# Sums of weight tiles started one item sooner, with one written order for VectorE's weight work

## The chip, the cores and the metric

The kernel runs on one core of a Trainium2 chip. The metric is the device time of one launch in microseconds, lower is better; times are medians over runs of the same kernel.

## The reference

A decoder trunk of two layers over x, 256 tokens of 2048 features in f32. Layer 0 uses differential attention, layer 1 latent attention; each layer then attends into 256 memory tokens and ends with a squared-ReLU MLP, which is the place of the change:

```python
def sq_relu_mlp(h, wup, wdown):        # wup 2048 x 8192, wdown 8192 x 2048
    return jnp.square(jax.nn.relu(h @ wup)) @ wdown

for i in range(2):
    x = x + attention_i(rms_norm(x, attn_norm[i]))
    x = x + memory_cross_attention(rms_norm(x, cross_norm[i]), mem_h, ca_wq[i], ca_wkv[i], ca_wo[i])
    x = x + sq_relu_mlp(rms_norm(x, mlp_norm[i]), mlp_wup[i], mlp_wdown[i])
return rms_norm(x, final_norm)
```

## The kernel before

**Three matmuls for one.** Every large product is made of three TensorE passes in the type fp32r. A weight tile and an activation tile are each split into a hi part (a cast to fp32r) and a lo part (what the cast lost); the passes are hi by hi, hi by the weights' lo, and the activations' lo by hi. Activations split in this way lie in "units", tiles of 128 partitions by hi and lo by 4 x 256 numbers, from the pool `units` with 13 places.

**The way of a weight tile.** All weights come in tiles of 1 MB, 128 partitions by 2048 f32 numbers (`raw`, pool `wraw`, 6 places of 8 KB in a partition; a unit takes 8 KB too). SP's queue issues the loads, in the order in which the program writes them (L165). ScalarE casts a half of a tile (128x1024) to `whi` (L193), and VectorE subtracts it from the raw half to make `wlo` (L194). There are four buffers for each of these two halves. So a tile needs two casts and two lo parts, and TensorE uses each half as soon as its lo part is there.

**The list of tiles.** `plan` is the list of all tiles in the order of their use. `take()` hands the next one to TensorE's code and calls `fill()`, which keeps four items written ahead: for each it writes the load, the casts and the lo parts into the program.

**The MLP.** The 8192 hidden columns are cut into 8 blocks of 1024. Block 0 is multiplied by the up weights in the plain way. Blocks 1 to 7 go through `Seven`: a block is seen as 2 x 2 blocks of smaller matrices, and seven products of sums of blocks replace eight plain products. They are worked in the order p1, p5, p3, p7, p2, p6, p4. A product takes two tiles, x = 0 and 1, of 12 matmuls each. The sums on the side of the activations are made by `Forms` and don't change here. Those on the side of the weights are made in the raw tiles themselves:

- p1, p3 and p2 use a fetched tile as it is (block 00, 11 or 10 of the up weights).
- p5 uses p1's tile plus a newly fetched one (block 01), and p7 uses p3's tile plus that same one. These two sums are VectorE's (L758, one instruction of 128x2048, in place). They are called "the sums" below: two tiles, two products, seven blocks and two layers make 56.
- p6 and p4 use what p7 and p6 leave, and add a block by a DMA that accumulates in place, issued from POOL's queue (L764) after the lo parts of p7 or p6.

**The order of the items.** `mlp_line` weaves tiles of the down projection between those of the products, and each down tile feeds 24 matmuls. The pattern is first tile of a product, second tile, down tile. In blocks 2 to 6 there is one more down tile between the two tiles of p3. The last product of a block, p4, is held back and stands between p1 and p5 of the next block, as a pair of its own with its down tile. A product's matmuls write PSUM banks named `pr`, those of the down projection `mm`.

**What sets the order on each engine.** TensorE's instructions stay as the program writes them. For the other engines a list scheduler sets the order when the kernel is built, from a model of durations: among the instructions whose inputs it reckons ready it takes those written first. Instructions under `keep_in_program_order` (loads, accumulating DMAs, the sums) keep their written order in their own queue. The lo parts are not so tied. Once built, each engine works strictly in its order.

Of the kernel before, what the change touches and what calls it, by code (L numbers as in the profile page):

```python
# [14 lines left out]
ALU = mybir.AluOpType  # L15
# [6 lines left out]
CH = 512  # L22
EPS = 1e-6
WARM = 13
RAWS = 6
MLP_BLOCKS = 8
SEVEN = (1, 2, 3, 4, 5, 6, 7)
EVS = 7
# [17 lines left out]
def trunk(ctx, tc, x, xT, mem, memT, positions, gcols, gfinal, lam_vecs, consts, W, out):  # L46
    nc = tc.nc

    def pool(name, bufs, space=None):
        kw = {"space": space} if space else {}  # L50
        return ctx.enter_context(tc.tile_pool(name=name, bufs=bufs, **kw))

    keep = pool("keep", 1)
    wraw = pool("wraw", RAWS)
    whalf = pool("whalf", 4)
    units = pool("units", 13)
    work = pool("work", 2)
    small = pool("small", 3)
    banks = pool("banks", 8, bass.MemoryType.PSUM)
# [3 lines left out]
    def nm(s):  # L63
        serial[0] += 1
        return f"{s}_{serial[0]}"
# [13 lines left out]
    class Task:  # L79
# [9 lines left out]
        def step(self):  # L89
            try:  # L90
                d = next(self.gen)
            except StopIteration:
                self.done = True
                side.remove(self)
                return
            if isinstance(d, Task):
                self.waits = d
            else:
                self.waits = None
                self.ready = clock[0] + d  # L100
# [60 lines left out]
    def f32(ap):  # L161
        return ap.bitcast(F32)
# [2 lines left out]
        tc.keep_in_program_order((queue or nc.sync).dma_start(dst, src))  # L165


    stream = []

    def raw_tile():  # L170
        return wraw.tile([P, 4 * CH], F32, tag="raw", name=nm("raw"))
# [1 line left out]
    def split_weights(src, width, pieces=2, loads=1, queue=None):  # L173
        raw = raw_tile()
        n = 4 * width
        m = n // loads
        for i in range(loads):
            load(raw[:, i * m : (i + 1) * m], src[:, i * m : (i + 1) * m], queue)
        return halves_of(raw, n, pieces)

    class split_pieces:
# [4 lines left out]
        def next(self):  # L186
            m, i = self.m, self.i
            at = i * m % (self.n // 2)
            if at == 0:
                self.halves.append([whalf.tile([P, 2 * CH], F32R, tag=tag, name=nm(tag)) for tag in ("whi", "wlo")])  # L190
            hi, lo = (w[:, at : at + m] for w in self.halves[-1])
            r = self.raw[:, i * m : (i + 1) * m]
            nc.scalar.copy(hi, r)  # L193
            nc.vector.tensor_tensor(lo, r, f32(hi), ALU.subtract)  # L194
            self.i += 1

    def halves_of(raw, n=4 * CH, pieces=2):
# [4 lines left out]

    plan = []
    ready = []
    AHEAD = 4

    def fill():
        while len(ready) < AHEAD and plan:
            job = plan.pop(0)
            if callable(job):  # L210
                ready.append(job())
            else:
                name, i, width = job
                ready.append(split_weights(W[name][i, :, : 4 * width], width))
# [4 lines left out]
    def take():  # L219
        fill()  # L220
        got = ready.pop(0)
        fill()
        taken[0] += 1
        if taken[0] in hooks:
            hooks[taken[0]]()
        return got
# [496 lines left out]
    class Seven:  # L723
# [18 lines left out]
            return raw  # L742

        def job(self, p, x):
            def run():
                r, other = self.raw, None
                if p in self.B:
                    o = r[p, x] = self.fetch(*self.B[p], x)
                elif p == "p5":
                    o, other = r.pop(("p1", x)), self.fetch(0, 1, x)  # L750
                    r["12", x] = other
                elif p == "p7":
                    o, other = r.pop(("p3", x)), r.pop(("12", x))
                else:
                    o = r.pop((p, x))
                split = split_pieces(o, 4 * CH, 2)
                if other is not None:
                    tc.keep_in_program_order(nc.vector.tensor_tensor(o, o, other, ALU.add))  # L758
                for _ in range(2):
                    split.next()  # L760
                if p in self.ADDED:
                    after, block = self.ADDED[p]
                    r[after, x] = o
                    add = nc.gpsimd.dma_start(o, self.source(*block, x), accum_op=ALU.add)  # L764
                    tc.keep_in_program_order(add)
                return split.halves

            return run

        def items(self):  # L770
# [611 lines left out]
def build(a, w):  # L1382
    import concourse.bacc as bacc

    nc = bacc.Bacc("TRN2", target_bir_lowering=False, num_devices=1, dynamic_dma_scratch_size=1024)
    arrays = {}

    def dram(name, v):
        arrays[f"in_{name}_dram"] = v
        return nc.dram_tensor(f"in_{name}_dram", v.shape, mybir.dt.from_np(v.dtype), kind="ExternalInput").ap()  # L1390

    args = [dram(k, a[k]) for k in ("x", "xT", "mem", "memT", "positions", "gcols", "gfinal", "lam_vecs", "consts")]
    weights = {k: dram(k, v) for k, v in w.items()}
    o = nc.dram_tensor("out_0_dram", (S, D), F32, kind="ExternalOutput").ap()
    with tile.TileContext(nc, schedule_with_timeline_sim=True) as tc, tc.manual_schedule(engines={mybir.EngineType.PE}):
        trunk(tc, *args, weights, o)
    return nc, arrays
# [8 lines left out]
```

## Time and profile before

| | |
|---|---|
| median of 3 runs (lowest to highest) | 2247.47 us (2247.27 to 2249.18) |
| the profiled execution, and its span | 2249.26 us, 2247.5 us |
| granted TensorE clock, mean | 0.998 |
| TensorE matmul / weight load busy | 2228.2 us (99%) / 1853.7 us (82%) |
| VectorE busy | 1675.6 us (75%) |
| ScalarE busy | 1354.6 us (60%) |
| GpSimd busy | 153.9 us (7%) |
| moved from and to memory | 484.09 MB, 215 GB/s on average |

Three groups of instructions belong to the weights:

```profile
L194 DVE TENSOR_TENSOR wlo<-raw,whi 128x1024 fp32r<-128x1024 f32 (+2 forms) x962 | 1154.6, 1213 | 483.6 <-ACT whi L193 455.2
L193 ACT CAST whi<-raw 128x1024 fp32r<-128x1024 f32 (+2 forms) x962 | 993.6, 1041 | 754.5 <-PE mm L155 530.9
L758 DVE TENSOR_TENSOR raw<-raw,raw 128x2048 f32<-128x2048 f32 x56 | 127.9, 2284 | 0.0
```

Such a row names line, engine and operation, what is written from what, how many there are, then the busy time in us and the mean of one in ns, and last the idle time of the engine just ahead of them and what ended most of it. PE is TensorE, PEld its loading of the stationary operand, DVE is VectorE, ACT ScalarE, POOL GpSimd, SP the queue that issues the loads. In a row of the timeline the first two numbers are start and length in us, xN says that N instructions stand in the row, and the bracket names an idle time ahead of it and what ended that. In a row of the waits stand the engine that waited and for what, then us in total, number of waits and the longest.

### The profile page before, as it was taken

To read this page: it belongs to the slowest core of one execution; us is meant where nothing else is said; L and a number is where in the kernel's file an instruction comes from. 1 tells how busy PE (TensorE), PEld (TensorE's weight loads), DVE (VectorE), ACT (ScalarE), POOL (GpSimd) and SP (SyncE) were. 2 spreads that over 40 slices of the span, in tenths; PEclk is the share of its full clock that TensorE was granted. 3 is DMA by queue.
4 is the path that set the end of the run, shared out by engine and by line. 5 is a ranking of instruction groups with operands and counts; after the bars stand their busy time and mean duration, and the time that the engine had idled before them with its cause. 6 is when DMAs were issued, how large, how long until landed. Compare 5 with 4: busy or idle time off the path is not lost.

```text
span 2247.5 us, 27444 instructions
## 1 busy us (share of the span) xinstructions
PE 2228.2 (99%) x10521; PEld 1853.7 (82%) x10521; DVE 1675.6 (75%) x1836; ACT 1354.6 (60%) x1815; POOL 153.9 (7%) x250
## 2 busy tenths in 40 slices
PE   9999999999999999999999999999999999999998
PEld 7888888888888888888889888888888888888786
DVE  6665647678888788788765766778887887887864
ACT  6544645666666666656655755566666666666664
POOL 0210110000000000000000311000000000000001
PEclk9999999999999999999999999999999999999999
DMA  9446555435877877876955334643688678678692
GB/s 364 157 143 210 193 197 206 152 129 206 262 250 254 244 249 255 244 249 219 297 176 180 116 141 150 243 150 132 216 255 277 222 250 275 223 250 276 221 306 75
DMA packets 73716, 484.09 MB, mean 215 GB/s; under 512 B 8432, under 2 KB 8816, under 8 KB 18032
## 3 DMA queue, kind: packets, MB, share of 16 engines
q1 hardware_dynamic: 64944, 422.56, 50.9%
q0 software_dynamic: 8064, 58.72, 13.1%
q8 instruction: 82, 1.34, 0.2%
q10 hardware_dynamic: 576, 1.05, 0.2%
q14 instruction: 50, 0.41, 0.1%
HBM read 480.20 MB, written 2.10 MB: 215 GB/s over the span
## 4 chain that ended last, share of the span: by engine, by line
PE 92%; DVE 5%; ACT 2%; issue 1%; DMA 0%; ACTq 0%; POOLq 0%
PE mm L155 66%; PE pr L155 20%; PE ax L155 3%; PE ax L159 2%; DVE wlo L194 2%; DVE raw L758 2%; ACT whi L193 1%; PE mm L159 1%; DVE unit L289 0%; DMA raw<-in_da_wqkv_dram 0%; DVE x L438 0%; DVE unit L316 0%; ACT ev L1078 0%; DVE unit L487 0%; DVE os L658 0%
## 5 line engine op out<-in xcount | busy, mean ns | idle before, releaser
L194 DVE TENSOR_TENSOR wlo<-raw,whi 128x1024 fp32r<-128x1024 f32 (+2 forms) x962 | 1154.6, 1213 | 483.6 <-ACT whi L193 455.2
L193 ACT CAST whi<-raw 128x1024 fp32r<-128x1024 f32 (+2 forms) x962 | 993.6, 1041 | 754.5 <-PE mm L155 530.9
L155 PE MATMUL mm<-whi,unit 128*128 128x512 f32 (+3 forms) x4544 | 1444.0, 389 | 2.6 <-ACT unit L315 1.7
L155 PEld LDWEIGHTS mm<-whi,unit 128*128 128x128 f32 x4544 | 850.1, 188 | 169.2 <-ACT unit L315 2.7
L155 PE MATMUL mm<-wlo,unit 128*128 128x512 f32 (+3 forms) x2272 | 878.3, 387 | 2.2 <-DVE wlo L194 2.2
L155 PE MATMUL pr<-whi,unit 128*128 128x512 f32 x1568 | 502.9, 391 | 0.0
L155 PEld LDWEIGHTS mm<-wlo,unit 128*128 128x128 f32 x2272 | 428.0, 188 | 85.6 <-DVE wlo L194 7.2
L155 PEld LDWEIGHTS pr<-whi,unit 128*128 128x128 f32 x1568 | 294.4, 188 | 61.3 <-ACT whi L193 0.5
L155 PE MATMUL pr<-wlo,unit 128*128 128x512 f32 x784 | 307.3, 392 | 3.0 <-DVE wlo L194 2.7
L155 PEld LDWEIGHTS pr<-wlo,unit 128*128 128x128 f32 x784 | 147.2, 188 | 39.5 <-DVE wlo L194 9.5
L758 DVE TENSOR_TENSOR raw<-raw,raw 128x2048 f32<-128x2048 f32 x56 | 127.9, 2284 | 0.0
L764 POOL DMA_DIRECT2D raw<-in_mlp_wup_dram x56 | 49.4, 882 | 1125.6 <-DVE wlo L194 990.3
L438 DVE TENSOR_TENSOR x<-x,mm 128x512 f32<-128x512 f32 x152 | 100.0, 682 | 9.4 <-PE mm L155 8.7
L328 POOL TENSOR_TENSOR rs<-rs,mhalf 128x1 f32<-128x1 f32 (+1 forms) x28 | 23.5, 844 | 681.5 <-DVE rs L327 681.5
L288 ACT CAST unit<-ax 128x512 fp32r<-128x512 f32 (+1 forms) x88 | 48.9, 567 | 30.1 <-PE ax L159 27.7
L289 DVE TENSOR_TENSOR unit<-ax,unit 128x512 fp32r<-128x512 f32 (+1 forms) x88 | 57.4, 661 | 3.0 <-ACT unit L288 1.3
L500 ACT ACTIVATE p<-ax,nmax 128x256 f32<-128x256 f32 (+1 forms) x80 | 33.6, 428 | 30.0 <-DVE nmax L498 29.5
L322 ACT ACTIVATE junk<-x 128x512 bf16<-128x512 f32 x56 | 35.2, 628 | 9.4 <-DVE x L438 8.4
L155 PE MATMUL ax<-unit,unit 128*128 128x256 f32 (+1 forms) x240 | 37.2, 281 | 0.0
L155 PEld LDWEIGHTS ax<-unit,unit 128*128 128x128 f32 x240 | 34.3, 190 | 2.5
L155 PE MATMUL ax<-raw,unit 128*128 128x256 f32 (+1 forms) x240 | 35.3, 279 | 0.8 <-ACT unit L486 0.6
L155 PEld LDWEIGHTS ax<-raw,unit 128*128 128x128 f32 x240 | 32.0, 190 | 2.4 <-ACT unit L486 1.0
(150 smaller groups left out, 925.8 us busy)
## 6 DMA issues: line engine op xcount, KB each, us to landing
raw<-in_mlp_wup_dram SPq DMA_DIRECT2D x128, 1024.0 KB, 5.0
raw<-in_mlp_wdown_dram SPq DMA_DIRECT2D x128, 1024.0 KB, 7.0
raw<-in_mlp_wup_dram POOLq DMA_DIRECT2D x56, 1024.0 KB, 11.0
raw<-in_da_wqkv_dram SPq DMA_DIRECT2D x45, 1024.0 KB, 5.0
raw<-in_da_wo_dram SPq DMA_DIRECT2D x16, 1024.0 KB, 4.9
raw<-in_ca_wkv_dram SPq DMA_DIRECT2D x16, 1024.0 KB, 4.9
raw<-in_mla_wo_dram SPq DMA_DIRECT2D x16, 1024.0 KB, 5.0
raw<-in_ca_wq_dram SPq DMA_DIRECT2D x8, 1024.0 KB, 5.1
```

Of the source, the lines that this page charges most:

```text
L155: return nc.tensor.matmul(o, stationary, moving, start=start, stop=stop, skip_group_check=not alone)
L159: nc.tensor.transpose(o, src, ident)
L193: nc.scalar.copy(hi, r)
L194: nc.vector.tensor_tensor(lo, r, f32(hi), ALU.subtract)
L288: nc.scalar.copy(hi, src)
L289: nc.vector.tensor_tensor(dst[:, 1, :n, t * P : (t + 1) * P], src, f32(hi), ALU.subtract)
L322: nc.scalar.activation(junk[:, : src.shape[1]], src, AF.Square, accum_out=acc)
L328: nc.gpsimd.tensor_tensor(r[:, :n], r[:, :n], mhalf.broadcast_to([P, n]), ALU.pow)
L438: nc.vector.tensor_tensor(xc, xc, ps, ALU.add)
L500: nc.scalar.activation(pr[:, i * w : (i + 1) * w], sb[:, i * w : (i + 1) * w], AF.Exp, bias=nmax[:, i : i + 1], accum_out=ssum[:, i : i + 1],)
L758: tc.keep_in_program_order(nc.vector.tensor_tensor(o, o, other, ALU.add))
L764: add = nc.gpsimd.dma_start(o, self.source(*block, x), accum_op=ALU.add)
```

## The change

It has four parts.

1. An item of `Seven` is cut in two. `begin()` fetches its tile and writes the sum, `run()` the casts, the lo parts and the accumulating DMA. `fill()` calls `begin()` of the next item before it writes the current one. So a product's load and sum stand one item sooner in the program; for the second tile of p5 and p7 that is ahead of the first tile's casts and lo parts, and for the first tile ahead of the preceding down tile's load, casts and lo parts.
2. Every lo part and every sum gets the same issue order token, "weights" (`in_turn`). All lo parts and sums then have one order among themselves on VectorE, the written one; before, the sums had one only among themselves.
3. `wraw` has 7 places instead of 6.
4. `units` has 12 places instead of 13, so the two pools together take the same room.

```diff
-RAWS = 6
+RAWS = 7
...
-    units = pool("units", 13)
+    units = pool("units", 12)
...
+    def in_turn(ins):
+        tc.stamp_issue_order_token(ins.ins, "weights")
+        return ins
...
             nc.scalar.copy(hi, r)
-            nc.vector.tensor_tensor(lo, r, f32(hi), ALU.subtract)
+            in_turn(nc.vector.tensor_tensor(lo, r, f32(hi), ALU.subtract))
             self.i += 1
...
     def fill():
         while len(ready) < AHEAD and plan:
             job = plan.pop(0)
+            if callable(job) and job not in begun:
+                job.begin()
+            if plan and callable(plan[0]):
+                begun.append(plan[0])
+                plan[0].begin()
             if callable(job):
                 ready.append(job())
...
         def job(self, p, x):
-            def run():
+            def begin():
                 r, other = self.raw, None
                 if p in self.B:
-                    o = r[p, x] = self.fetch(*self.B[p], x)
+                    r[p, x] = self.fetch(*self.B[p], x)
                 elif p == "p5":
-                    o, other = r.pop(("p1", x)), self.fetch(0, 1, x)
+                    r[p, x], other = r.pop(("p1", x)), self.fetch(0, 1, x)
                     r["12", x] = other
                 elif p == "p7":
-                    o, other = r.pop(("p3", x)), r.pop(("12", x))
-                else:
-                    o = r.pop((p, x))
+                    r[p, x], other = r.pop(("p3", x)), r.pop(("12", x))
+                if other is not None:
+                    in_turn(nc.vector.tensor_tensor(r[p, x], r[p, x], other, ALU.add))
+
+            def run():
+                o = self.raw[p, x]
                 split = split_pieces(o, 4 * CH, 2)
-                if other is not None:
-                    tc.keep_in_program_order(nc.vector.tensor_tensor(o, o, other, ALU.add))
                 for _ in range(2):
                     split.next()
                 if p in self.ADDED:
                     after, block = self.ADDED[p]
-                    r[after, x] = o
+                    self.raw[after, x] = o
                     add = nc.gpsimd.dma_start(o, self.source(*block, x), accum_op=ALU.add)
                     tc.keep_in_program_order(add)
                 return split.halves
 
+            run.begin = begin
             return run
```

By the added lines the lo part's line becomes L196, the sum's L763, and the lines behind them move likewise (L289 is L297, L793 is L803). TensorE's and POOL's orders are unchanged.

**VectorE at p5 of block 2 (layer 0), before.** Here and in the next two places `raw` is a weight tile, `whi` and `wlo` its halves, `unit` a down tile's activations, `u` a row of sums of products; numbers are the kernel's own names, which differ between the two kernels. raw_5109 is p5's first tile, raw_5144 its second, raw_5261 the down tile ahead of p5:

```order
L194 TENSOR_TENSOR wlo_5246<-raw_4799,whi_5245 128x1024
L289 TENSOR_TENSOR unit_5192<-ax_5329,unit_5192 128x4x128
L758 TENSOR_TENSOR raw_5144<-raw_5144,raw_5337 128x2048
L194 TENSOR_TENSOR wlo_5264<-raw_5261,whi_5263 128x1024
L194 TENSOR_TENSOR wlo_5268<-raw_5261,whi_5267 128x1024
L758 TENSOR_TENSOR raw_5109<-raw_5109,raw_5287 128x2048
L793 TENSOR_TENSOR u_1009_5188<-pr_5336,u_1009_5188 128x512
L194 TENSOR_TENSOR wlo_5291<-raw_5109,whi_5290 128x1024
```

The same place in the change, where raw_5081 is p5's first tile, raw_5111 its second and raw_5264 the down tile:

```order
L196 TENSOR_TENSOR wlo_5246<-raw_4766,whi_5245 128x1024
L763 TENSOR_TENSOR raw_5081<-raw_5081,raw_5261 128x2048
L297 TENSOR_TENSOR unit_5192<-ax_5332,unit_5192 128x4x128
L196 TENSOR_TENSOR wlo_5267<-raw_5264,whi_5266 128x1024
L196 TENSOR_TENSOR wlo_5271<-raw_5264,whi_5270 128x1024
L763 TENSOR_TENSOR raw_5111<-raw_5111,raw_5290 128x2048
L803 TENSOR_TENSOR u_1009_5188<-pr_5339,u_1009_5188 128x512
L196 TENSOR_TENSOR wlo_5294<-raw_5081,whi_5293 128x1024
```

The two sums keep their two places but for one row, and change them with each other: the first tile's stands ahead of the down tile's lo parts, the second tile's behind them.

**VectorE at p7 of block 1, before.** raw_4764 is p7's first tile, raw_4799 its second, raw_4821 the down tile ahead of p7:

```order
L194 TENSOR_TENSOR wlo_4806<-raw_4799,whi_4805 128x1024
L194 TENSOR_TENSOR wlo_4824<-raw_4821,whi_4823 128x1024
L194 TENSOR_TENSOR wlo_4828<-raw_4821,whi_4827 128x1024
L758 TENSOR_TENSOR raw_4764<-raw_4764,raw_4674 128x2048
L289 TENSOR_TENSOR unit_4880<-ax_4930,unit_4880 128x4x128
L194 TENSOR_TENSOR wlo_4847<-raw_4764,whi_4846 128x1024
L194 TENSOR_TENSOR wlo_4851<-raw_4764,whi_4850 128x1024
L758 TENSOR_TENSOR raw_4799<-raw_4799,raw_4717 128x2048
L289 TENSOR_TENSOR unit_4880<-ax_4967,unit_4880 128x4x128
L194 TENSOR_TENSOR wlo_4888<-raw_4799,whi_4887 128x1024
```

And in the change, where the three tiles are raw_4740, raw_4766 and raw_4822:

```order
L196 TENSOR_TENSOR wlo_4806<-raw_4766,whi_4805 128x1024
L763 TENSOR_TENSOR raw_4740<-raw_4740,raw_4633 128x2048
L196 TENSOR_TENSOR wlo_4825<-raw_4822,whi_4824 128x1024
L196 TENSOR_TENSOR wlo_4829<-raw_4822,whi_4828 128x1024
L763 TENSOR_TENSOR raw_4766<-raw_4766,raw_4677 128x2048
L196 TENSOR_TENSOR wlo_4848<-raw_4740,whi_4847 128x1024
L196 TENSOR_TENSOR wlo_4852<-raw_4740,whi_4851 128x1024
L297 TENSOR_TENSOR unit_4881<-ax_4932,unit_4881 128x4x128
L196 TENSOR_TENSOR wlo_4888<-raw_4766,whi_4887 128x1024
```

The first sum moves ahead of the down tile's two lo parts, the second ahead of the first tile's two.

**VectorE at p5 of block 1, before.** The down tile ahead of p5 is raw_4633; the sums are of raw_4556, p5's first tile, and raw_4590, its second:

```order
L289 TENSOR_TENSOR unit_4625<-ax_4667,unit_4625 128x4x128
L758 TENSOR_TENSOR raw_4556<-raw_4556,raw_4674 128x2048
L194 TENSOR_TENSOR wlo_4593<-raw_4590,whi_4592 128x1024
L289 TENSOR_TENSOR unit_4625<-ax_4703,unit_4625 128x4x128
L194 TENSOR_TENSOR wlo_4597<-raw_4590,whi_4596 128x1024
L194 TENSOR_TENSOR wlo_4636<-raw_4633,whi_4635 128x1024
L758 TENSOR_TENSOR raw_4590<-raw_4590,raw_4717 128x2048
```

And in the change, where the three tiles are raw_4636, raw_4510 and raw_4558:

```order
L297 TENSOR_TENSOR unit_4625<-ax_4670,unit_4625 128x4x128
L196 TENSOR_TENSOR wlo_4593<-raw_4558,whi_4592 128x1024
L297 TENSOR_TENSOR unit_4625<-ax_4706,unit_4625 128x4x128
L196 TENSOR_TENSOR wlo_4597<-raw_4558,whi_4596 128x1024
L763 TENSOR_TENSOR raw_4510<-raw_4510,raw_4633 128x2048
L196 TENSOR_TENSOR wlo_4639<-raw_4636,whi_4638 128x1024
L196 TENSOR_TENSOR wlo_4643<-raw_4636,whi_4642 128x1024
L763 TENSOR_TENSOR raw_4558<-raw_4558,raw_4677 128x2048
```

The first tile's sum moves from ahead of four lo parts to between the two of p1's second tile and the two of the down tile.

**On the other queues.** On SP the loads of the tiles that p1, p5 and p3 fetch stand ahead of the load of the down tile that they used to follow. On ScalarE the casts keep their order but for a few rows.

More of the change, by code (lines that the diff above doesn't have):

```diff
@@ L165, in load @@
         tc.keep_in_program_order((queue or nc.sync).dma_start(dst, src))
-    stream = []
+    def in_turn(ins):
+        tc.stamp_issue_order_token(ins.ins, "weights")
+        return ins
     def raw_tile():
@@ L204, in trunk @@
     ready = []
+    begun = []
     AHEAD = 4
```

## The prediction

> **What bounds the kernel now.** I read the busy times first, then who waited for whom, then TensorE's rows at the places of waiting, and last VectorE's rows ahead of them.
>
> ```profile
> PE 2228.2 (99%) x10521; PEld 1853.7 (82%) x10521; DVE 1675.6 (75%) x1836; ACT 1354.6 (60%) x1815; POOL 153.9 (7%) x250
> ...
> 536.77 5.44 PE pr L155 x24
> ```
>
> TensorE is busy for 99% of the span, and the change leaves its order of 10521 matmuls as it is. So the only thing to win is time in which a matmul comes late. The second row, from the chain of waits, gives the measure: 24 matmuls in 5.44 us, one every 0.227 us. What lies between two starts beyond 0.227 us is lost.
>
> ```profile
> PEld pr L155 <- DVE wlo L194: 9.5, 16, 1.1
> PEld mm L155 <- DVE wlo L194: 7.2, 12, 0.6
> ```
>
> These are the waits that concern the change (us in total, times, longest): TensorE waits 28 times for a lo part of weights. All 28 lie in the two MLPs, 14 in each. In TensorE's timeline they have four forms, named A to D here, one example of each:
>
> ```profile
> 621.83 0.39 PE L155 MATMUL mm<-whi,unit 128*128 128x512 f32 x1
> 622.40 0.50 PE L155 MATMUL mm<-wlo,unit 128*128 128x512 f32 x1 [0.18 <-DVE wlo L194]
> 622.74 0.63 PE L155 MATMUL mm<-whi,unit 128*128 128x512 f32 x2
> ...
> 627.76 0.39 PE L155 MATMUL pr<-whi,unit 128*128 128x512 f32 x1
> 628.16 0.50 PE L155 MATMUL pr<-wlo,unit 128*128 128x512 f32 x1
> 628.50 0.63 PE L155 MATMUL pr<-whi,unit 128*128 128x512 f32 x2
> ...
> 572.70 0.74 PE L155 MATMUL pr<-whi,unit 128*128 128x512 f32 x2
> 574.20 0.50 PE L155 MATMUL pr<-wlo,unit 128*128 128x512 f32 x1 [0.76 <-DVE wlo L194]
> 574.54 0.63 PE L155 MATMUL pr<-whi,unit 128*128 128x512 f32 x2
> ...
> 1072.09 0.39 PE L155 MATMUL pr<-whi,unit 128*128 128x512 f32 x1
> 1073.09 0.50 PE L155 MATMUL pr<-wlo,unit 128*128 128x512 f32 x1 [0.61 <-DVE wlo L194]
> 1073.43 0.63 PE L155 MATMUL pr<-whi,unit 128*128 128x512 f32 x2
> ```
>
> A: the down tile ahead of product p5, 0.57 - 0.227 = 0.34 us, and the matmul behind it another 0.34 - 0.227 = 0.11: 0.45 us. B: p5's own first lo part, 0.40 - 0.227 = 0.17, and 0.11: 0.28 us. C: the second tile of p7 in block 1, 574.20 - (572.70 + 2 x 0.227) = 1.05, and 0.11: 1.15 us. D: the first tile of p7 in block 7, 1.00 - 0.227 = 0.77, and 0.11: 0.89 us. A and B come once in each of blocks 2 to 7, 12 times each in two layers (the 12 of the mm row are A); C and D come twice each (with B the 16 of the pr row). Together 5.4 + 3.4 + 2.3 + 1.8 = 12.9 us: more than this the change can't bring.
>
> **The place of A and B.** VectorE's rows in block 2, and the one of ScalarE that answers:
>
> ```profile
> 617.18 1.23 DVE L194 TENSOR_TENSOR wlo<-raw,whi 128x1024 fp32r<-128x1024 f32 x1 [1.50 <-ACT whi L193]
> 618.33 0.69 DVE L289 TENSOR_TENSOR unit<-ax,unit 128x512 fp32r<-128x512 f32 x1
> 618.93 2.28 DVE L758 TENSOR_TENSOR raw<-raw,raw 128x2048 f32<-128x2048 f32 x1
> 621.13 2.35 DVE L194 TENSOR_TENSOR wlo<-raw,whi 128x1024 fp32r<-128x1024 f32 x2
> 623.40 2.29 DVE L758 TENSOR_TENSOR raw<-raw,raw 128x2048 f32<-128x2048 f32 x1
> 625.60 0.69 DVE L793 TENSOR_TENSOR u<-pr,u 128x512 f32<-128x512 f32 x1
> 626.88 3.50 DVE L194 TENSOR_TENSOR wlo<-raw,whi 128x1024 fp32r<-128x1024 f32 x3 [0.59 <-ACT whi L193]
> ...
> 625.79 2.95 ACT L193 CAST whi<-raw 128x1024 fp32r<-128x1024 f32 x3 [5.43 <-DVE raw L758]
> ```
>
> A row starts 0.08 us before the one ahead of it ends (618.93 + 2.28 = 621.21, next start 621.13), so in a full queue a sum takes 2.20, a lo part 1.14, a unit or u3 row 0.60. The first sum (618.93) is of p5's second tile, the second (623.40) of its first tile: the order is crossed. ScalarE therefore sits idle for 5.43 us until 625.79 and only then casts the first tile.
>
> In the change the first tile's sum comes first, at the end of the lo part of 617.18, so at 618.33; the unit row follows at 620.53, the down tile's lo at 621.13, as before. **A stays** at 0.45 us: the same 2.20 and 0.60 stand ahead of that lo part. The cast of p5's first tile no longer waits for the second sum: its own ended at 620.6, its half buffers are free once TensorE has left them, some 1.4 us (6 x 0.227) after each half of the product ahead. So behind the second sum (623.40) and u3 (625.60) its lo part starts at 626.20 instead of 626.88 and ends at 627.43; TensorE wants it at 627.76 + 0.227 = 627.99. **B goes**, with 0.5 us to spare: 12 x 0.28 = 3.4 us. The second tile's cast waits for the sum that now ends at 625.7, and comes when the first tile's came before. The unit row, 2.2 us later, has nobody near it: it feeds a down tile of the next triples.
>
> **Blocks 1 and 7** have no down tile between the two tiles of p3, so the sums meet other rows:
>
> ```profile
> 559.65 1.23 DVE L194 TENSOR_TENSOR wlo<-raw,whi 128x1024 fp32r<-128x1024 f32 x1 [1.50 <-ACT whi L193]
> 563.78 2.29 DVE L758 TENSOR_TENSOR raw<-raw,raw 128x2048 f32<-128x2048 f32 x1
> 564.48 0.40 PE L155 MATMUL mm<-wlo,unit 128*128 128x512 f32 x1
> ...
> 1062.50 2.59 DVE L194 TENSOR_TENSOR wlo<-raw,whi 128x1024 fp32r<-128x1024 f32 x2 [1.50 <-ACT whi L193]
> 1066.88 0.39 PE L155 MATMUL mm<-wlo,unit 128*128 128x512 f32 x1
> ...
> 537.89 2.59 DVE L194 TENSOR_TENSOR wlo<-raw,whi 128x1024 fp32r<-128x1024 f32 x2 [0.64 <-ACT whi L193]
> 542.27 0.39 PE L155 MATMUL mm<-wlo,unit 128*128 128x512 f32 x1
> ```
>
> C: p7's first sum moves from 563.78 to the end of the lo part of 559.65, at 560.80. The down tile's lo parts then start at 563.00 and 564.15; the first ends at 564.23, 0.25 us before TensorE takes it (564.48). The second sum follows at 565.3, p7's four lo parts from 567.5 on; the last that was late starts near 570.4 instead of 572.92. **C goes**: 2 x 1.15 = 2.3 us.
>
> D: the first sum goes behind the first of the two lo parts of 1062.50, at 1063.64, and the down tile's lo runs from 1065.84 to 1067.06. TensorE starts 0.05 us after the end of a late lo part (622.35 and 622.40 above), so at 1067.12 instead of 1066.88: 0.24 late, and 0.11. The second sum is over at 1070.4, p7's lo starts at 1070.3 instead of 1071.81, in time. **D shrinks** from 0.89 to 0.35: 2 x 0.54 = 1.1 us.
>
> E, new: p5 in block 1. Its first sum stood far ahead, before the lo parts quoted last; now it stands behind the first of the two lo parts of 537.89, at 539.04, and the down tile's lo runs from 541.24 to 542.46, for a matmul that started at 542.27: 0.25 late, and 0.11. **E costs** 2 x 0.36 = 0.7 us.
>
> For D and E the bounds are nothing (a cast or lo part a little earlier) and what stands now: D as it is, E as much as A.
>
> **p7 in blocks 2 to 6**, where nothing waited:
>
> ```profile
> 727.75 1.23 DVE L194 TENSOR_TENSOR wlo<-raw,whi 128x1024 fp32r<-128x1024 f32 x1
> 733.19 3.95 DVE L194 TENSOR_TENSOR wlo<-raw,whi 128x1024 fp32r<-128x1024 f32 x3 [1.50 <-ACT whi L193]
> 734.85 0.39 PE L155 MATMUL mm<-wlo,unit 128*128 128x512 f32 x1
> 740.29 0.39 PE L155 MATMUL pr<-wlo,unit 128*128 128x512 f32 x1
> ```
>
> The first sum now follows the lo part of 727.75 (728.90 to 731.18); the down tile's lo ends at 732.3 for 734.85. The second sum follows the first row of the three from 733.19 (734.34 to 736.6); p7's first lo ends at 737.8 for 740.29. 2.5 us are left of 4.5: cost nothing.
>
> **Places and units.** Each load of such a tile now stands one item earlier in SP's queue, ahead of a down tile's load, and the seventh place pays for it. A unit place fewer: in the compiled program I looked for the shortest time between the last read of a unit and the first write of its successor in the same place.
>
> ```profile
> 327.98 0.62 PE L155 MATMUL mm<-whi,unit 128*128 128x512 f32 x2
> 374.34 0.51 ACT L315 ACTIVATE unit<-raw,g 128x256 fp32r<-128x256 f32 x1
> ...
> raw<-in_mlp_wdown_dram SPq DMA_DIRECT2D x128, 1024.0 KB, 7.0
> ...
> 713.59 0.33 SPq L165 DMA_DIRECT2D raw<-in_mlp_wdown_dram  x1
> 721.22 1.06 ACT L193 CAST whi<-raw 128x1024 fp32r<-128x1024 f32 x1 [0.81 <-PE mm L155]
> ```
>
> With twelve it is 374.34 - 328.4 = 46 us: cost nothing. The tightest load is issued at 713.59 and cast at 721.22, 7.6 us for a landing of 7.0; the place it takes comes free at the same row in both kernels.
>
> **Sum.** -3.4 - 2.3 - 1.1 + 0.7 = -6.1 us. The profiled execution took 2249.26 (span 2247.5), so 2243.2 for such a one; the median of the runs is 2247.47, 1.8 below it, so **2241.4**, 0.27% less. With the bounds of D and E the gain is 4.8 (D unchanged, E 0.45) to 7.5 (neither): 2240.0 to 2242.7.
>
> The Trainium skill speaks against the close packing used here: VectorE: DVE Perf Modes, section "The DRAIN you can't avoid", says that the next operation does not start until the pipe is empty, though one that nothing holds starts earlier. The rows above start 0.08 us before the end of the one ahead; by the strict reading D and E would be two joins of 0.08 later at four places, 0.6 us, and the gain 5.5.
>
> **Rivals.** (1) *B stays.* If ScalarE can't cast p5's first tile earlier, because it is held by half buffers and not by the sum, its lo part starts at 626.88 again. Against it: the idle time before the cast of 625.79 is put down to the sum. Gain 6.1 - 3.4 = 2.7: 2244.8. Chance 0.24. (2) *A goes too*, if the sum ahead of the down tile can start before 618.33, by a cast ahead that comes earlier. For it: VectorE idles 1.50 us before the lo part of 617.18. Against it: that idle time is ScalarE's, which waits for TensorE. Gain 6.1 + 5.4 = 11.5: 2236.0. Chance 0.10. (3) *Slower: the down tile's load comes late.* SP works in order; a load asked for one item sooner that finds no free place holds the down load behind it, and VectorE, in its fixed order, then holds everything behind that lo part. It begins when the 0.6 us between landing and cast and A's missing slack are used up; 1 us late in each of 12 blocks is +12 - 6.1 = +5.9: 2253.4. For it: 7.6 us is the smallest lead there is in the MLP. Against it: that load's place is no later, and the others have seven to choose from. Chance 0.11. (4) *It does nothing*: TensorE's waits reappear one row later, because the sums take as long as before: 2247.5. Chance 0.05, for the crossed order of the sums is gone for certain.
>
> **The numbers.** Chance of the forecast 0.50. About 0.2% (4.5 us) is what a measurement of this kernel can tell from no change. Faster by more: forecast and rival 2, 0.60; within: rivals 1 and 4, 0.29; slower: rival 3, 0.11. The range from 2236.0 to 2247.0 takes in rivals 1 and 2 and leaves out 3 and 4, 0.16.
>
> **What would show it.** TensorE's waits for lo parts fall from 28 to 16: 12 of form A at 0.57 us between starts, and D and E, two each, near 0.47. No wait of a pr matmul at p5's first tile, and ScalarE no longer idle for 5 us ahead of its cast. p7 in blocks 2 to 6 without a wait. It is wrong if A is gone or longer, if p7's lo parts are late in every block, or if a load or a unit stands among what TensorE waits for.

## The result

The changed kernel takes **2240.68 us** (median of 7 runs, 2240.15 to 2242.6) against 2247.47 us before (median of 7 runs, 2246.95 to 2249.18). The ratio is 0.9970, with a 95% interval of 0.9961 to 0.9980: 6.8 us less. The prediction was 2241.4 us.

The profiled execution took 2240.68 us, with a span of 2238.8. First its busy times, then from the view of waits the line of TensorE's weight loads that waited for a lo part (us in total, times, longest; L196 is L194 of before):

```profile
PE 2221.9 (99%) x10521; PEld 1852.5 (83%) x10521; DVE 1675.2 (75%) x1836; ACT 1365.4 (61%) x1815; POOL 154.1 (7%) x250
```

```profile
PEld mm L155 <- DVE wlo L196: 9.7, 17, 0.6
```

VectorE does as much as before (1675.2 against 1675.6 us busy), and only its order differs. The 16 waits in rows of `pr` are gone altogether. Of the 17 in rows of `mm`, one lies at the kernel's start (at 14.62 us); the other 16 are the 12 of form A, two of E and two of what D became.

**Where the time went.** The same matmul can be found in both traces, since TensorE's order is the same. Three of them, from TensorE's timeline: ahead of the first MLP, between the two, and behind the second. Before:

```profile
510.93 0.62 PE L155 MATMUL mm<-whi,unit 128*128 128x512 f32 x2
...
1156.30 0.39 PE L155 MATMUL mm<-wlo,unit 128*128 128x512 f32 x1
...
2187.96 0.62 PE L155 MATMUL mm<-whi,unit 128*128 128x512 f32 x2
```

And in the changed kernel:

```profile
509.25 0.62 PE L155 MATMUL mm<-whi,unit 128*128 128x512 f32 x2
...
1151.27 0.39 PE L155 MATMUL mm<-wlo,unit 128*128 128x512 f32 x1
...
2179.56 0.62 PE L155 MATMUL mm<-whi,unit 128*128 128x512 f32 x2
```

The lead grows from 1.68 to 5.03 us over the first MLP and to 8.40 over the second. So **the MLPs won 3.35 and 3.37 us, 6.7 together**; between them the lead stays at 5.01 to 5.03 for all matmuls. The 1.68 us ahead of them come from the first 17 us and are no part of the change (last section).

**The places A to E in the changed kernel**, TensorE's rows in order of time: E (block 1, with the rows behind it), C (block 1), A and B (block 2), and the down tile ahead of p7 in block 7:

```profile
540.36 0.39 PE L155 MATMUL mm<-whi,unit 128*128 128x512 f32 x1
540.83 0.50 PE L155 MATMUL mm<-wlo,unit 128*128 128x512 f32 x1
541.17 0.64 PE L155 MATMUL mm<-whi,unit 128*128 128x512 f32 x2
...
542.34 0.39 PE L155 MATMUL mm<-wlo,unit 128*128 128x512 f32 x1
...
571.43 0.62 PE L155 MATMUL pr<-whi,unit 128*128 128x512 f32 x2
571.89 0.39 PE L155 MATMUL pr<-wlo,unit 128*128 128x512 f32 x1
...
619.36 0.39 PE L155 MATMUL mm<-whi,unit 128*128 128x512 f32 x1
619.93 0.50 PE L155 MATMUL mm<-wlo,unit 128*128 128x512 f32 x1 [0.18 <-DVE wlo L196]
...
625.28 0.39 PE L155 MATMUL pr<-whi,unit 128*128 128x512 f32 x1
625.51 0.39 PE L155 MATMUL pr<-wlo,unit 128*128 128x512 f32 x1
...
1062.13 0.39 PE L155 MATMUL mm<-whi,unit 128*128 128x512 f32 x1
1062.59 0.50 PE L155 MATMUL mm<-wlo,unit 128*128 128x512 f32 x1
```

A stands as it was, 0.57 us between the two starts. B and C run at 0.23 us a matmul, and D's old place, p7's first tile, is not among the waits any more. E and the down tile ahead of p7 in block 7 are new and small, 0.47 and 0.46 us.

VectorE at p5 of block 2, and ScalarE's casts that answer (the first is of p5's first tile, the second of its second tile):

```profile
614.72 1.23 DVE L196 TENSOR_TENSOR wlo<-raw,whi 128x1024 fp32r<-128x1024 f32 x1 [1.50 <-ACT whi L195]
615.86 2.28 DVE L763 TENSOR_TENSOR raw<-raw,raw 128x2048 f32<-128x2048 f32 x1
618.06 0.69 DVE L297 TENSOR_TENSOR unit<-ax,unit 128x512 fp32r<-128x512 f32 x1
618.66 2.35 DVE L196 TENSOR_TENSOR wlo<-raw,whi 128x1024 fp32r<-128x1024 f32 x2
620.93 2.29 DVE L763 TENSOR_TENSOR raw<-raw,raw 128x2048 f32<-128x2048 f32 x1
...
623.73 8.15 DVE L196 TENSOR_TENSOR wlo<-raw,whi 128x1024 fp32r<-128x1024 f32 x7
```

```profile
618.25 1.06 ACT L195 CAST whi<-raw 128x1024 fp32r<-128x1024 f32 x1 [0.36 <-PE pr L155]
...
623.33 1.06 ACT L195 CAST whi<-raw 128x1024 fp32r<-128x1024 f32 x1 [2.66 <-DVE raw L763]
```

The first tile is cast at 618.25, 0.11 us after its sum is over (615.86 + 2.28 = 618.14); by the bracket the last thing that the cast waited for was TensorE, not the sum. Its lo part starts at 623.73, straight behind a row of L803 (a row of sums of products, left out here), and is over at 624.95 for a matmul at 625.51. Before, ScalarE stood idle for 5.43 us at this place and the lo part came late.

### The profile page after: what moved, and what is told of

Same layout as the page of the kernel before. It is cut to its first block, busy times and chain, and to the rows that moved or that the text cites. A ratio compares the mean times of both kernels' runs of the same rounds, so it can differ in the third digit from the quotient of the medians.

```text
span 2238.8 us, 27416 instructions
## 1 busy us (share of the span) xinstructions
PE 2221.9 (99%) x10521; PEld 1852.5 (83%) x10521; DVE 1675.2 (75%) x1836; ACT 1365.4 (61%) x1815; POOL 154.1 (7%) x250
## 4 chain that ended last, share of the span: by engine, by line
PE 94%; DVE 4%; ACT 1%; issue 1%; DMA 0%; ACTq 0%; POOLq 0%; DVEq 0%
PE mm L155 68%; PE pr L155 20%; PE ax L155 3%; PE ax L159 2%; DVE raw L763 2%; DVE wlo L196 1%; PE mm L159 1%; ACT whi L195 1%; DVE unit L297 0%; DMA raw<-in_da_wqkv_dram 0%; DVE x L446 0%; DVE unit L324 0%; DVE unit L495 0%; DVE os L666 0%; ACT unit L579 0%
## 5 line engine op out<-in xcount | busy, mean ns | idle before, releaser
L196 DVE TENSOR_TENSOR wlo<-raw,whi 128x1024 fp32r<-128x1024 f32 (+2 forms) x962 | 1155.7, 1213 | 473.7 <-ACT whi L195 444.1
L763 DVE TENSOR_TENSOR raw<-raw,raw 128x2048 f32<-128x2048 f32 x56 | 127.9, 2284 | 0.0
L297 DVE TENSOR_TENSOR unit<-ax,unit 128x512 fp32r<-128x512 f32 (+1 forms) x88 | 57.5, 662 | 4.4 <-ACT unit L296 1.3
```

The source lines that it names most:

```text
L196: in_turn(nc.vector.tensor_tensor(lo, r, f32(hi), ALU.subtract))
L297: nc.vector.tensor_tensor(dst[:, 1, :n, t * P : (t + 1) * P], src, f32(hi), ALU.subtract)
L763: in_turn(nc.vector.tensor_tensor(r[p, x], r[p, x], other, ALU.add))
```

## The experiments

Two questions were open. Which of the change's four parts brings the 6.7 us? And is A, the largest wait that is left, set by the sum ahead of it on VectorE, or by the half buffers, that is by ScalarE, which casts a half only when TensorE has left a buffer? The runs share their runs of the kernel before in two groups: 2247.83 us (9 runs) for e1 to e4, 2247.51 us (17 runs) for e5 to e7.

### e1: without the sum ahead of A

```diff
-                if other is not None:
+                if other is not None and (p, x) != ("p5", 0):
                     in_turn(nc.vector.tensor_tensor(r[p, x], r[p, x], other, ALU.add))
```

> The changed kernel without the sums of p5's first tile (14 of the 56 are left out, so p5 works with p1's tile alone). The question is what makes the down tile's first lo part ahead of p5 late (form A, 12 times, still there after the change) and the same place of block 1 (E, twice). Theory: the sum of p5's first tile that VectorE does just ahead of it. Then A and E are gone, TensorE's rows there follow each other at 0.23 us, and the time falls by 12 x 0.45 + 2 x 0.36 = 6.1 us to 2234.6 (2233.5 to 2235.5). Rival: the half buffers set it (ScalarE casts that half only when TensorE has left a buffer). Then A and E stay, and the time is that of the change, 2240.7 (2240 to 2241.5).

Measured: 2234.22 us (2233.51 to 2234.51), ratio 0.9940 (0.9925 to 0.9955). TensorE at A in block 2:

```profile
619.14 0.39 PE L155 MATMUL mm<-whi,unit 128*128 128x512 f32 x1
619.36 0.39 PE L155 MATMUL mm<-wlo,unit 128*128 128x512 f32 x1
```

0.22 us between the starts: A is gone in all twelve blocks, and E with it. Of the lo parts only D's two places and the one at the start are still waited for. The changed kernel's own rows speak against the half buffers too: the second of the down tile's two casts is over by 617.90, and the lo parts start at 618.66, straight behind the sum and the unit row.

```profile
616.84 1.06 ACT L195 CAST whi<-raw 128x1024 fp32r<-128x1024 f32 x1 [0.33 <-PE pr L155]
```

So **A is the sum's**, as the prediction had it. Its rival 2 (A can go) saw that an earlier sum would remove A; what the change lacks is a way to start that sum sooner.

### e2: the first tile's sum half an item sooner

The sum of the first tile of p5 and p7 is written between the two lo parts of the tile ahead of the down tile. `begun` keeps it from being written twice.

```diff
-            if plan and callable(plan[0]):
+            if plan and callable(plan[0]) and plan[0] not in begun:
                 begun.append(plan[0])
                 plan[0].begin()
...
-                for _ in range(2):
-                    split.next()
+                split.next()
+                if len(plan) > 1 and callable(plan[1]) and not callable(plan[0]):
+                    begun.append(plan[1])
+                    plan[1].begin()
+                split.next()
```

> The changed kernel, with the sum of a product's first tile (p5 and p7) written half an item sooner still: between the two lo parts of the tile ahead of the down tile. The order of the loads stays. VectorE was idle for 1.50 us ahead of that second lo part, waiting for its cast. Theory: most of the sum falls into that idle time, the lo part behind it has 2 us before TensorE takes it, and the down tile's lo part comes in time. A, D and E all go: 12 x 0.45 + 4 x 0.36 = 6.8 us, 2233.9 (2233 to 2235). Rival 1: the second lo part of the tile ahead is now late in the place of the down tile's: 2240.7, with TensorE's waits on pr matmuls. Rival 2: the sum's second operand has not landed half an item sooner, and VectorE stands still behind it: slower than the change by 1 us or more at each of 14 places, 2255.

Measured: 2233.71 us (2233.05 to 2235.18), ratio 0.9939 (0.9924 to 0.9954). VectorE at p5 of block 2, TensorE at the down tile, and TensorE's waits for lo parts in the whole kernel:

```profile
612.45 2.28 DVE L763 TENSOR_TENSOR raw<-raw,raw 128x2048 f32<-128x2048 f32 x1
...
616.39 2.35 DVE L196 TENSOR_TENSOR wlo<-raw,whi 128x1024 fp32r<-128x1024 f32 x2
```

```profile
618.68 0.39 PE L155 MATMUL mm<-whi,unit 128*128 128x512 f32 x1
618.90 0.39 PE L155 MATMUL mm<-wlo,unit 128*128 128x512 f32 x1
```

```profile
PEld mm L155 <- DVE wlo L196: 0.5, 1, 0.5
```

The sum fills the 1.50 us in which VectorE had waited for a cast, and the down tile's first lo part starts at 616.39 and is over about 1.2 us later, more than 1 us ahead of its matmul. The one wait that is left is that at the kernel's start. The MLPs have none: against the changed kernel each wins another 3.7 us (by the starts of the same matmuls). Both rivals fall: neither the second lo part of the tile ahead nor the sum's second operand comes late.

### e3: the change without the earlier writing

```diff
-            if plan and callable(plan[0]):
-                begun.append(plan[0])
-                plan[0].begin()
```

> The change without the earlier writing: fixed order, seven raw places and twelve units are kept, and the sum stands again right ahead of its own tile's lo parts. Theory: the time of writing is what counts. The down tile's lo part goes ahead (A and B are gone), but the second tile's sum now ends only when its cast should begin, and its lo part comes 1.0 to 1.5 us late, as in form C, at all 28 second tiles of p5 and p7 instead of at 2. With about 0.15 for the matmuls behind it that is 28 x 1.15 to 1.65 = 32 to 46, less the 13 us of A to D: 2267 to 2280, best value 2272. Rival: the fixed order is what brings the gain: 2241. Second rival: the order of the sums doesn't matter: 2247.5.

Measured: 2290.34 us (2289.67 to 2291.35), ratio 1.019 (1.0175 to 1.0206), outside the expected 2267 to 2280. First TensorE's waits, then in block 2 VectorE's row of the second tile's sum and the lo parts behind it, ScalarE's cast between them, and TensorE at that tile:

```profile
PEld pr L155 <- DVE wlo L196: 30.1, 28, 1.1
PEld pr L155 <- ACT whi L195: 28.6, 28, 1.3
```

```profile
629.87 2.28 DVE L760 TENSOR_TENSOR raw<-raw,raw 128x2048 f32<-128x2048 f32 x1
633.32 6.90 DVE L196 TENSOR_TENSOR wlo<-raw,whi 128x1024 fp32r<-128x1024 f32 x6 [1.17 <-ACT whi L195]
```

```profile
632.24 4.88 ACT L195 CAST whi<-raw 128x1024 fp32r<-128x1024 f32 x5 [2.45 <-DVE raw L760]
```

```profile
632.33 0.39 PE L155 MATMUL pr<-whi,unit 128*128 128x512 f32 x1
633.34 0.51 PE L155 MATMUL pr<-whi,unit 128*128 128x512 f32 x1 [0.62 <-ACT whi L195]
634.60 0.50 PE L155 MATMUL pr<-wlo,unit 128*128 128x512 f32 x1 [0.75 <-DVE wlo L196]
```

The places were the expected ones, all 28 second tiles, but a place costs more. I had priced only the late lo part. Here the cast is late too: TensorE waits for the hi half first (1.01 - 0.227 = 0.78 us) and then again for the lo part, which can begin only behind that cast (1.26 - 0.227 = 1.03). With the matmuls behind it such a place costs 1.95 us; in the two of p7 in block 1 only the lo part is late (1.2 us). 26 x 1.95 + 2 x 1.2 = 53 us. Against e2, which has no such wait, the MLPs of this profile are 28.9 and 26.9 us longer by the starts of the same matmuls, 55.8 together: two places cost 2.2 and one 3.9. At that last one TensorE's clock fell (last section).

So **the time of writing is the change's core.** The fixed order without it (and with the changed rooms, which e5 shows to be worth nothing) is worse than the kernel before by 43 us: there the scheduler had pulled the sums ahead by itself, crossed as they were.

### e4: six raw places, thirteen units

```diff
-RAWS = 7
+RAWS = 6
-    units = pool("units", 12)
+    units = pool("units", 13)
```

> The change with the old room: six raw places and thirteen units. Order of all engines as in the change but for some 19 rows. Theory: the seventh place keeps loads in time, but few depend on it. Worked from the change's trace with a place fewer, eleven loads of each MLP are issued 5.8 us ahead of their first use, against landings of 5 to 7 us: they come up to 1.2 us late, and most of that is hidden between the cast and TensorE's use. 2243 (2240.5 to 2249), with waits for casts whose tile has not landed. Rival: the load that comes late holds VectorE's fixed order and everything behind it: 22 places of 1 us or more, 2262. Second rival: the place is worth nothing, 2240.7.

Measured: 2240.64 us (2240.11 to 2242.55), ratio 0.9971 (0.9958 to 0.9983): the changed kernel's time, as the second rival had it. A down tile's load in block 2, on SP's queue in the changed kernel:

```profile
615.97 0.33 SPq L165 DMA_DIRECT2D raw<-in_mlp_wdown_dram  x1
```

The same load in this one, how long it took to land (the last number, us), and its first cast:

```profile
620.81 0.33 SPq L165 DMA_DIRECT2D raw<-in_mlp_wdown_dram  x1
```

```profile
raw<-in_mlp_wdown_dram SPq DMA_DIRECT2D x1, 1024.0 KB, 4.8
```

```profile
626.61 1.05 ACT L195 CAST whi<-raw 128x1024 fp32r<-128x1024 f32 x1 [0.23 <-PE pr L155]
```

With a place fewer the load goes out 4.8 us later, 5.8 us ahead of its cast, as I had worked out. This one lands in 4.8, and its cast waits for TensorE and not for it. Not every load does so well. Four casts of this run wait for the load of a down tile; the changed kernel has no such wait. Here is their row of the waits, and the longest of them in ScalarE's timeline:

```profile
ACT whi L195 <- DMA raw<-in_mlp_wdown_dram: 4.7, 4, 1.7
```

```profile
634.73 1.05 ACT L195 CAST whi<-raw 128x1024 fp32r<-128x1024 f32 x1 [1.66 <-DMA raw<-in_mlp_wdown_dram]
```

So the late loads that the theory expected are there, but none of them reaches TensorE: it waits for the same 17 lo parts as in the changed kernel, and the two MLPs are as long as there to within 0.02 us by the starts of the same matmuls. The theory was right that such waits come, and wrong about their number and their price. The seventh place buys a longer lead, which ScalarE uses at four casts and TensorE nowhere.

### e5: the places alone

The kernel before with seven raw places and twelve units.

> The kernel before with seven raw places and twelve units, and nothing else of the change. Theory: neither place is waited for, so the rooms alone are worth nothing: 2247.5 (2246.5 to 2248.5), with the waits A to D as before. Rival: a place fewer among the units holds a unit's writing back: slower by 1 us or more, with TensorE's waits for units grown. Second rival: the seventh raw place brings a part of the gain: 2245 or less.

Measured: 2247.74 us (2246.98 to 2248.34, 10 runs), ratio 1.0001 (0.9991 to 1.0010). The places alone are worth nothing, in either direction, and twelve units are enough.

### e6: without the fixed order

```diff
-            in_turn(nc.vector.tensor_tensor(lo, r, f32(hi), ALU.subtract))
+            nc.vector.tensor_tensor(lo, r, f32(hi), ALU.subtract)
...
-                    in_turn(nc.vector.tensor_tensor(r[p, x], r[p, x], other, ALU.add))
+                    tc.keep_in_program_order(nc.vector.tensor_tensor(r[p, x], r[p, x], other, ALU.add))
```

> The change without the fixed order (no token; each sum is only kept behind the one instruction written ahead of it on VectorE). 24 rows on VectorE stand elsewhere: at p7 in blocks 2 to 6 the second sum follows the first directly, ahead of the down tile's lo parts, and at p5 in block 1 it stands between the down tile's two. Theory: the earlier writing alone brings the gain. The down tile's lo part at p7 had 2.5 us and now keeps 0.3, so nothing is late: 2240.7 (2240 to 2241.7). Rival: the 2.2 us of the second sum are too much there, and 10 places are late by 0.2 to 0.5 us with 0.15 behind it: 2244 to 2247.

Measured: 2241.52 us (2241.12 to 2242.36), ratio 0.9973 (0.9963 to 0.9984): 0.84 us more than the changed kernel's median, at the upper end of what was expected. p7 in blocks 2 to 6, which I had priced, has no wait. What I had not priced is the other place, p5 in block 1, where the second sum stands between the down tile's two lo parts. TensorE there:

```profile
543.48 0.61 PE L155 MATMUL mm<-whi,unit 128*128 128x512 f32 x2
544.42 0.50 PE L155 MATMUL mm<-wlo,unit 128*128 128x512 f32 x1 [0.32 <-DVE wlo L196]
```

The second lo part comes 544.42 - (543.48 + 2 x 0.227) = 0.49 us late, once in each MLP. So the fixed order brings something like 1 us of the 6.8 (the MLPs are 0.53 and 0.59 us longer by the starts of the same matmuls), and the earlier writing the rest.

### e7: only the time of writing, half an item further

e2 without the fixed order and with six raw places and thirteen units: of the whole change only the earlier writing is left.

> The version in which the first tile's sum is written between the two lo parts of the tile ahead of the down tile, with six raw places, thirteen units and no fixed order. On VectorE 43 rows stand elsewhere than in that version with token and seven places: at p5 in block 1, and at p7 in blocks 2 to 6, the second sum goes between the down tile's two lo parts. Theory: only the time at which the sums are written counts: 2233.7 (2233 to 2235), no wait of TensorE for a lo part. Rival: without the token or the place one of the waits comes back: 2236 to 2241.

Measured: 2233.64 us (2233.13 to 2234.32), ratio 0.9938 (0.9923 to 0.9953), the same as e2; its profile too shows one wait for a lo part, that at the start. e2 and e7 beat the kernel before by 14.1 and 13.9 us, and the changed one by 7.0.

## Why the prediction was right

By its own steps:

- **Nothing to win but late matmuls.** Right: between the MLPs the two traces keep the same distance to 0.02 us.
- **A stays.** Right to the digit, 0.57 us between the starts, and for the reason given: e1 and e2 remove it by taking the sum from ahead of that lo part.
- **B goes.** Right. The forecast had 0.5 us to spare, and the rows show about as much (624.95 for 625.51). Worth 12 x 0.34 = 4.1 us by the starts of the same matmuls (0.29 to 0.36 each), not 3.4.
- **C goes.** Right, worth 1.19 and 1.21, 2.4 us for 2.3.
- **D shrinks, E appears.** Right, at 0.46 and 0.47 us between starts, where 0.47 was forecast. D's net gain was 0.50 in each MLP (0.54 forecast), E cost 0.41 and 0.39 (0.36 forecast).
- **The sum** was 6.1 and came out at 6.7 in the traces. What was sized too small is the tail of a late matmul. I counted the late one and the one behind it (0.11 us). The next ones are a little slow as well: behind E five matmuls take 542.34 - 541.17 = 1.17 us instead of 5 x 0.227 = 1.135, and over about ten it comes to 0.01 to 0.06 us for each wait. The same tail makes the prediction's ceiling of 12.9 us too low: without any of the 28 waits, in e2, the MLPs are 14.1 us shorter than before by the starts of the same matmuls.
- **Seven places and twelve units cost nothing.** Right (e5), and the seventh place brings nothing either (e4).
- **The Trainium skill's strict reading** (VectorE: DVE Perf Modes, "The DRAIN you can't avoid") would have made D and E 0.08 us later at each join and the gain 5.5. The rows after the change still start 0.08 us before the end of the one ahead (615.86 + 2.28 against 618.06), and E came at the 0.47 of the other reading.

**The rivals.** B did not stay (1). A did not go (2), though e2 shows how it can: by a sum written earlier, not by an earlier cast. No load came late (3): in the changed kernel's MLPs no cast and no sum waits for one. Nor was it as near as the rival feared: with a place fewer (e4) four casts do wait, by up to 1.66 us, and TensorE feels none of it. That it does nothing (4) is out by the interval of the ratio.

**What was wrong in the words.** I called 7.6 us the smallest lead of a load in the MLP. A tile that p5 adds was issued at 612.5 us before and read by the sum at 618.93, a lead of 6.4; the 7.6 counts casts only. In the change that one has 13.6 (607.3 to 620.93), so the change eased the tightest load. And the description of the kernel said that the sums keep their written order among themselves; the rows quoted there show the second tile's sum ahead of the first tile's. These rows fit a rule that holds an instruction behind the one written just ahead of it on its engine, which need not be the other sum; no run tests that rule by itself. The forecast used the rows and not that sentence.

## What to carry to other kernels

Where one engine is busy for 99% and the engine that feeds it for 75%, look for long instructions of the feeder that stand just ahead of a short one that is wanted soon, and move the long one into an idle time of the feeder that the trace shows; e2's half item was worth as much as the whole change. When a sum's result must pass two more steps before it is used (here a cast on ScalarE and a subtraction on VectorE), count that whole chain: with the sum written late, the cast and the lo part were late one behind the other, and a place cost 1.95 us where the lo part alone suggested 1.2. Take a change apart before keeping all of it: of four parts one carried nearly everything, and the fixed order without that one cost 43 us.

## What the hardware showed beyond that

The two profiles differ by 1.7 us before any weight sum is done. Windows of the first 16 us, before and then after (window, length, busy us of TensorE, its weight loads, VectorE, ScalarE and GpSimd, granted clock, DMA share, GB/s):

```profile
8.00:16.00 8.00, 6.62 (x22) 4.96 (x22) 6.25 (x11) 7.11 (x15) 0.00 (x0) 0.79 1.01 394
```

```profile
8.00:16.00 8.00, 6.92 (x28) 5.13 (x29) 6.82 (x12) 7.56 (x15) 0.00 (x0) 1.00 1.01 387
```

In the profile of before the granted clock fell to 0.79 in this window, and TensorE did 22 matmuls in it; after, it stayed at 1.00, and TensorE did 28. Of the seven experiments e3 alone shows 0.79 in the same window, the other six 1.00, e5 among them, which differs from the kernel before in two pool sizes alone. So it seems to follow the execution and not the kernel; with one profile of each kernel that is not shown outright. The Trainium skill says in TensorE: Matmul & The Clock Gate, Part 1, that the gate looks at a free-running window, so that the same kernel starts with a different number of slow matmuls from run to run; the 22 and 28 matmuls of the two windows fit that.

The clock also fell once in the middle of a kernel. In e3, at p7 of block 6 in the first MLP, TensorE waited for a hi half and then for its lo part, as everywhere in that run. Its rows just behind these waits, and a window over them:

```profile
1015.20 1.05 PE L155 MATMUL pr<-whi,unit 128*128 128x512 f32 x2
1016.05 0.63 PE L155 MATMUL pr<-wlo,unit 128*128 128x512 f32 x1
```

```profile
1015.00:1018.50 3.50, 3.50 (x10) 2.74 (x10) 3.23 (x4) 2.19 (x3) 0.88 (x1) 0.57 1.01 267
```

Two matmuls take 0.85 us there instead of 0.45, at a granted clock of 0.57, for some 3 us; this made the place 1.9 us dearer than the others. The same two waits stand at 25 other places of that run without such a price. Whether the waits brought it on at this one is not shown.

The matmul ahead of the first MLP that was shown above starts at 508.52 us (e5) to 511.51 us (e3) in the nine profiles. So a comparison of two single profiles carries up to 3.0 us from ahead of the MLPs, against an effect of 6.7, and the body of the kernel has to be compared by itself.
